# Output projection buffers in one pool laid out by the input projection's bytes, with the last products written in place

## The chip, the cores and the metric

The kernel runs on one core of a Trainium2 chip. The metric is device time in microseconds (us) of one execution; lower is better. The profile is one execution seen by the hardware profiler; its span runs from the first to the last instruction.

## The reference, cut to what matters

One layer over x of 512 tokens by 2048 channels, all in float32:

```python
proj = rmsnorm(x) @ w_in              # 512 x 6144: q, k, v, g_sb, x_lru, g_lru
y_sb  = stick_breaking_attention(q, k, v) * silu(g_sb)     # 8 heads x 128
y_lru = rg_lru(causal_conv(x_lru)) * silu(g_lru)           # 8 groups x 128
out = x + concat(y_sb, y_lru) @ w_out                      # 512 x 2048 @ 2048 x 2048
```

The mixer's result y has 16 tiles of 128 channels by 512 tokens: tiles 0 to 7 are the attention heads, 8 to 15 the recurrent (lru) groups.

## The kernel before, in words

Every matrix product is made from two-part numbers: an operand is split into a high part (cast to fp32r on ScalarE) and a low part (the difference, on VectorE), and three matmuls (high x high, high x low, low x high) stand for one.

**Input projection and mixer.** The loop over p = 0 to 3 takes two heads and two lru groups at a time. For each p three products run over the whole of x: `qk` (then the attention weights), `xg` (then the two lru groups) and `vg` (then `finish_vg`: gates and attention values). x is kept on chip, split, in 32 tiles xh0, xl0 to xh15, xl15 (64 KB of each partition); each of the twelve products reads them in the order 0 to 15, two pairs to a chunk, and `vg3` is the last. The gated results go to DRAM (`finish_y`, a store into `y_dram`), except heads 6 and 7, which are written straight into the buffer that the output projection reads.

**Four pools on the right side of the memory** belong to the input projection, from the edge inwards: xy (the x tiles, 64 KB), qk (split queries and keys, 18 KB), raw (weights as loaded, 16 KB), wsp (split weights, 16 KB). `proj.close()` gives them back, and the output projection's pools are put over the same bytes: c1 (8 tiles of w_out, 32 KB, at the edge), ya (4 tiles of y, 32 KB), wo (split weights, three of each part) and so (split y, six of each part). A tile of these waits only for the tiles whose bytes it takes (`reuse_waits="tile"`). As c1 and ya together are as large as xy, all the ya tiles lie over the second half of the x tiles.

**Output projection.** It is Strassen's: seven products p1, p3, p5, p7, p2, p6, p4 in this order, of 8 steps each (two column halves m by four depth pieces a). A step splits one piece of weights (`woh` on ScalarE, `wol` on VectorE, 128x1024), with m = 0 also a piece of y (`oh`, `ol`), and makes 12 matmuls of 512 columns (lines 602 to 604). The weight pieces are sums of two blocks of w_out: c1 and c2 are loaded (line 547), and after a step's split GpSimd issues an accumulating DMA (`add_c`, line 551) that adds the block that a later product wants. c2 is read by p3 and p7, then c3 takes its place for p2. p1 reads c1. The residual x comes in 16 loads from ScalarE's queue (line 616).

**Order of the loads.** SyncE's queue takes them in the order written: for a = 0 to 3 c1_0_a, c1_1_a and the two halves of ya_a (line 560), then the second half of ya3 (tiles 14 and 15, line 561), then the eight c2 loads. The order of an engine's instructions is fixed when the program is made (a scheduler with a model of the time places them); on the chip each engine runs its list in order. A DMA from SyncE or ScalarE also waits for an earlier one, as eight of them at most are under way.

Of the kernel before, what the change touches and what calls it, by code (L numbers as in the profile page):

```python
# [8 lines left out]
F32 = mybir.dt.float32  # L9
F32R = mybir.dt.float32r  # L10
# [3 lines left out]
ALU = mybir.AluOpType  # L14
# [7 lines left out]
def hybrid_block_kernel(ctx: ExitStack, tc: tile.TileContext, x, norm_gain, w_in, q_norm_gain,  # L22
# [20 lines left out]
    mixer, proj, heads = ExitStack(), ExitStack(), ExitStack()  # L43
    const = ctx.enter_context(tc.tile_pool(name="const", bufs=1))
    dram = ctx.enter_context(tc.tile_pool(name="dram", bufs=1, space=bass.MemoryType.DRAM))
    xy_pool = proj.enter_context(tc.tile_pool(name="xy", bufs=32, side="right"))
    qk_pool = proj.enter_context(tc.tile_pool(name="qk", bufs=2, side="right"))
    raw_pool = proj.enter_context(tc.tile_pool(name="raw", bufs=4, side="right"))
    wsp = proj.enter_context(tc.tile_pool(name="wsp", bufs=4, side="right"))
    v_pool = mixer.enter_context(tc.tile_pool(name="v", bufs=1))  # L50
# [114 lines left out]
    def prep_x(c, xt):  # L165
        for j in range(2):
            kt = 2 * c + j
            ps = ps_a.tile([P, 512], F32, tag="a", name=f"xp{kt}")
            for tt in range(TT):
                nc.tensor.transpose(ps[:, tt * P:(tt + 1) * P],  # L170
                                    xt[:, tt, j * P:(j + 1) * P], ident)
            h = xy_pool.tile([P, S], F32R, tag="xy", name=f"xh{kt}")
            l = xy_pool.tile([P, S], F32R, tag="xy", name=f"xl{kt}")
            evac_x[c] = nc.scalar.activation(h, ps, AF.Copy, scale=gain[:, kt:kt + 1])
            evac_l[kt] = nc.vector.scalar_tensor_tensor(out=l, in0=ps, scalar=gain[:, kt:kt + 1], in1=h.bitcast(F32),
                                           op0=ALU.mult, op1=ALU.subtract)
            xh.append(h)
            xl.append(l)
# [150 lines left out]
    def silu_gate(g, name):  # L329
        e = silu_sig(g, name, "se")  # L330
        nc.vector.tensor_tensor(out=g, in0=g, in1=e, op=ALU.mult)
        return g
# [1 line left out]
    y_dram = dram.tile([KT, P, S], F32, name="y_dram")  # L334
    late = {}

    def y_tile(k, name):

        if k in late:
            return late[k]  # L340
        return y_pool.tile([P, S], F32, tag="y", name=name)

    def finish_y(k, y):
        if k not in late:
            nc.sync.dma_start(y_dram[k], y)
    woff = [0, 512, 896, 1152]

    def attention_weights(h):
# [58 lines left out]
    def attention_values(h, wt, v, gate):  # L407
        hp = h % 2
        o = ps_a.tile([P, 512], F32, tag="a", name=f"o{h}")
        vh, vl, v3 = v  # L410
        wh, wl, w3 = wt
        hs = slice(hp * P, (hp + 1) * P)
        for kb in range(3):
            ws = slice(woff[kb], woff[kb] + S - 128 * kb)
            for a, b in ((vh, wh), (vh, wl), (vl, wh)):
                nc.tensor.matmul(o[:, 128 * kb:512], lhsT=a[:, kb, hs], rhs=b[:, ws],
                                 start=(kb == 0 and b is wh and a is vh), stop=False, skip_group_check=True)
        nc.tensor.matmul(o[:, 384:512], lhsT=v3[:, hs], rhs=w3, start=False, stop=True, skip_group_check=True)
        y = y_tile(h, f"y{h}")
        nc.vector.tensor_tensor(out=y, in0=o, in1=gate, op=ALU.mult)  # L420
        finish_y(h, y)

    def lru(g, xbank, gbank):
        n = f"l{g}"
# [47 lines left out]
        nc.scalar.activation(q, q, AF.Ln)  # L472
        nc.scalar.activation(q, q, AF.Exp, scale=0.5)
        nc.vector.tensor_tensor(out=ig, in0=ig, in1=q, op=ALU.mult)
        y = y_pool.tile([P, S], F32, tag="y", name=f"y{n}")
        nc.vector.tensor_tensor_scan(out=y, data0=r, data1=ig, initial=0.0, op0=ALU.mult, op1=ALU.add)
        gate = silu_gate(gbank, n)
        nc.vector.tensor_tensor(out=y, in0=y, in1=gate, op=ALU.mult)
        finish_y(8 + g, y)

    def finish_vg(p, banks, wts):
        vh = v_pool.tile([P, 3, 256], F32R, tag="vh", name=f"vh{p}")
        vl = v_pool.tile([P, 3, 256], F32R, tag="vl", name=f"vl{p}")
        v3 = v_pool.tile([P, 256], F32, tag="v3", name=f"v3{p}")
        for tt in range(TT):
            src = banks[tt // 2][:, (tt % 2) * 256:(tt % 2) * 256 + 256]
            r = rtok[:, tt:tt + 1]
            if tt == 3:  # L490
                nc.scalar.activation(v3, src, AF.Copy, scale=r)
                continue
            nc.scalar.activation(vh[:, tt, :], src, AF.Copy, scale=r)
            nc.vector.scalar_tensor_tensor(out=vl[:, tt, :], in0=src, scalar=r, in1=vh[:, tt, :].bitcast(F32),
                                           op0=ALU.mult, op1=ALU.subtract)
        v = (vh, vl, v3)
        gs = [evac(banks[2 + i], f"s{2 * p + i}") for i in range(2)]
        gates = [silu_gate(gs[i], f"s{2 * p + i}") for i in range(2)]
        for i in range(2):
            attention_values(2 * p + i, wts[i], v, gates[i])  # L500
# [32 lines left out]

    proj.close()
    NA = 4
    first = ExitStack()
    c1_pool = first.enter_context(tc.tile_pool(name="c1", bufs=8, side="right", reuse_waits="tile"))
    a_pool = first.enter_context(tc.tile_pool(name="ya", bufs=4, side="right", reuse_waits="tile"))
    wo_pool = first.enter_context(tc.tile_pool(name="wo", bufs=3, side="right", reuse_waits="tile"))
    so_pool = first.enter_context(tc.tile_pool(name="so", bufs=6, side="right", reuse_waits="tile"))  # L540

    w_out_a = w_out[0].rearrange("(b a s p) (h m n) -> s p a b h m n", p=P, s=2, a=NA, h=2, n=512)
    y_dram_a = y_dram.rearrange("(b a s) p t -> p a b s t", s=2, a=NA)

    def load_c(pool, tag, s, h, m, a, name):
        t = pool.tile([P, 2, 512], F32, tag=tag, name=name)
        nc.sync.dma_start(t, w_out_a[s, :, a, :, h, m, :])
        return t

    def add_c(t, s, h, m, a):  # L550
        nc.gpsimd.dma_start(t, w_out_a[s, :, a, :, h, m, :], accum_op=ALU.add)  # L551

    ya = [a_pool.tile([P, 2, 2, 512], F32, tag="ya", name=f"ya{a}") for a in range(NA)]
    c1 = {}
    for a in range(NA):
        for m in range(2):
            c1[m, a] = load_c(c1_pool, "c1", 0, 0, m, a, f"c1_{m}_{a}")
        if a < NA - 1:
            for b in range(2):
                nc.sync.dma_start(ya[a][:, b], y_dram_a[:, a, b])  # L560
    nc.sync.dma_start(ya[3][:, 1], y_dram_a[:, 3, 1])
    late[6], late[7] = ya[3][:, 0, 0, :], ya[3][:, 0, 1, :]
    finish_vg(3, banks, wts)

    mixer.close()
    heads.close()
# [4 lines left out]
                                          reuse_waits="tile"))  # L571

    def split_s(i, a, src):
        h = so_pool.tile([P, 2, 256], F32R, tag="sh", name=f"oh{i}_{a}")
        l = so_pool.tile([P, 2, 256], F32R, tag="sl", name=f"ol{i}_{a}")
        nc.scalar.copy(h, src)  # L576
        nc.vector.tensor_tensor(out=l, in0=src, in1=h.bitcast(F32), op=ALU.subtract)  # L577
        return h, l

    def product(i, pool, tag, src, w, after=None):  # L580


        out = {}
        s = []
        for m in range(2):
            for u in range(2):
                out[m, u] = pool.tile([P, 512], F32, tag=tag, name=f"p{i}_{m}{u}")
            for a in range(NA):
                if m == 0:
                    s.append(split_s(i, a, src[a]))  # L590
                sh, sl = s[a]
                wh = wo_pool.tile([P, 2, 512], F32R, tag="woh", name=f"woh{i}_{m}{a}")
                wl = wo_pool.tile([P, 2, 512], F32R, tag="wol", name=f"wol{i}_{m}{a}")
                nc.scalar.copy(wh, w[m, a])  # L594
                nc.vector.tensor_tensor(out=wl, in0=w[m, a], in1=wh.bitcast(F32), op=ALU.subtract)  # L595
                if after is not None:
                    after(m, a)
                for u in range(2):
                    us = slice(u * P, (u + 1) * P)
                    for j in range(2):  # L600
                        st, sp = a == 0 and j == 0, a == NA - 1 and j == 1
                        nc.tensor.matmul(out[m, u], lhsT=sh[:, j, us], rhs=wh[:, j, :], start=st, stop=False)  # L602
                        nc.tensor.matmul(out[m, u], lhsT=sh[:, j, us], rhs=wl[:, j, :], start=False, stop=False)  # L603
                        nc.tensor.matmul(out[m, u], lhsT=sl[:, j, us], rhs=wh[:, j, :], start=False, stop=sp)  # L604
        return out
# [27 lines left out]
    a12 = [t[:, :, 1, 0:256] for t in ya]  # L633
    a22 = [t[:, :, 1, 256:512] for t in ya]

    p1 = product(1, ps_mm, "mm", a11, c1, add_to(c1, 0, 1))
    c2 = {(m, a): load_c(c2_pool, "c2", 1, 1, m, a, f"c2_{m}_{a}") for m in range(2) for a in range(NA)}
    s7, s3 = [], []
    for a in range(NA):
        s7.append(sa_pool.tile([P, 2, 256], F32, tag="s7", name=f"s7_{a}"))  # L640
# [24 lines left out]
        tt(r22[k], r22[k], p5[k], ALU.subtract)  # L665

    p7 = product(7, ps_o, "o", s7, c2)
    c3 = {(m, a): load_c(c2_pool, "c2", 1, 0, m, a, f"c3_{m}_{a}") for m in range(2) for a in range(NA)}
    f = {}
    for k in MU:  # L670
        f[k] = res("f", f"f_{k[0]}{k[1]}")
# [21 lines left out]
    for k in MU:  # L693
        tt(r21[k], p4[k], r21[k])
        store(r21[k], 1, 0, *k)
    first.close()


# [27 lines left out]
```

## Time and profile before

| | |
|---|---|
| median of 3 runs | 808.15 us (808.1 to 809.76) |
| profiled execution | 807.12 us, span 805.4 us |
| TensorE busy | 776.2 us (96%), mean granted clock 0.985 |
| VectorE, ScalarE busy | 513.9 us (64%), 441.4 us (55%) |
| moved by DMA | 101.40 MB, mean 126 GB/s |

The medians are what is compared; the profiled execution is used for where the time goes. A share of busy time is a mean over stages with different limits, so the profile is read by stages.

### The profile page before, as it was taken

Reading aid. Unit: us, or ns where it says so; the run is one execution under the profiler, and the core shown is the slowest. Engines: PE = TensorE matmul, PEld = TensorE weight load, DVE = VectorE, ACT = ScalarE, POOL = GpSimd, SP = SyncE. Lnnn points to the kernel's source line nnn. Section 1 sums busy time; section 2 is a strip of 40 time slices with the busy share of each in tenths; the row PEclk is TensorE's granted clock in tenths of the full one; section 3 lists DMA queues with packets and bytes.
Section 4 is the critical chain, followed back from the end, with each engine's and each line's share of the span. In section 5 each row is a group of like instructions: output and inputs, shape, how many; then the busy total and the mean of one; then the engine's idle time right before and its main releaser. Section 6 shows DMA issues by size and latency. Waiting matters only on the chain.

```text
span 805.4 us, 10605 instructions
## 1 busy us (share of the span) xinstructions
PE 776.2 (96%) x3847; PEld 652.7 (81%) x3847; DVE 513.9 (64%) x857; ACT 441.4 (55%) x828; POOL 42.3 (5%) x55
## 2 busy tenths in 40 slices
PE   8999999999999999999999999999997488999997
PEld 7888889888888888888889888888996365788886
DVE  3665479772547788344589762548779466776794
ACT  5845577752447858225587742456866144545441
POOL 0000000000000000000000000000001033410220
PEclk9999999999999999999999999999999689999999
DMA  9522322232322222423222333322126999995492
GB/s 292 194 79 79 104 84 77 95 113 94 102 87 71 87 95 82 144 84 99 79 85 79 99 117 105 102 83 78 53 66 170 309 254 260 207 254 151 110 233 76
DMA packets 83240, 101.40 MB, mean 126 GB/s; under 512 B 5282, under 2 KB 61172, under 8 KB 83188
## 3 DMA queue, kind: packets, MB, share of 16 engines
q1 hardware_dynamic: 72180, 79.75, 30.7%
q0 software_dynamic: 8704, 16.78, 11.5%
q10 hardware_dynamic: 2304, 4.20, 1.6%
q8 instruction: 30, 0.49, 0.2%
q14 instruction: 22, 0.18, 0.1%
HBM read 92.84 MB, written 7.86 MB: 125 GB/s over the span
## 4 chain that ended last, share of the span: by engine, by line
PE 89%; DMA 9%; SPq 1%; DVE 0%; ACTq 0%; issue 0%; ACT 0%; DVEq 0%
PE p L603 5%; PE p L604 5%; PE p L602 5%; PE z L360 4%; DMA c<-in_w_out_dram 3%; DMA y_dram<-yl 3%; PE qk0b L282 2%; PE qk0b L283 2%; PE qk0b L284 2%; PE xg0b L283 2%; PE xg3b L284 2%; PE xg2b L284 2%; PE xg1b L284 2%; PE xg0b L284 2%; PE xg2b L282 2%; PE xg3b L282 2%
## 5 line engine op out<-in xcount | busy, mean ns | idle before, releaser
L602 PE MATMUL p<-woh,oh 128*128 128x512 f32 x224 | 82.9, 409 | 18.8 <-ACT oh L576 13.6
L594 ACT CAST woh<-c 128x1024 fp32r<-128x1024 f32 x56 | 58.7, 1049 | 68.4 <-PE p L604 41.6
L595 DVE TENSOR_TENSOR wol<-c,woh 128x1024 fp32r<-128x1024 f32 x56 | 68.2, 1222 | 42.9 <-ACT woh L594 42.9
L603 PE MATMUL p<-wol,oh 128*128 128x512 f32 x224 | 91.0, 406 | 3.6 <-DVE wol L595 3.6
L604 PE MATMUL p<-woh,ol 128*128 128x512 f32 x224 | 88.7, 401 | 0.0
L602 PEld LDWEIGHTS p<-woh,oh 128*128 128x128 f32 x224 | 43.5, 196 | 31.3 <-ACT oh L576 14.7
L603 PEld LDWEIGHTS p<-wol,oh 128*128 128x128 f32 x224 | 43.9, 196 | 16.3 <-DVE wol L595 7.3
L551 POOL DMA_DIRECT2D c<-in_w_out_dram x32 | 38.7, 1211 | 262.0 <-DVE ql L471 138.7
L604 PEld LDWEIGHTS p<-woh,ol 128*128 128x128 f32 x224 | 43.7, 195 | 9.2 <-DVE ol L577 0.2
L372 ACT ACTIVATE sp<-z 128x128 f32<-128x128 f32 (+3 forms) x32 | 13.9, 434 | 25.1 <-PE z L360 24.9
L283 PE MATMUL qk0b<-xl,hqk 128*128 128x512 f32 x64 | 26.4, 413 | 0.0
L284 PE MATMUL qk0b<-xh,lqk 128*128 128x512 f32 x64 | 25.2, 394 | 0.0
L283 PE MATMUL xg0b<-xl,hxg 128*128 128x512 f32 x64 | 25.2, 394 | 0.0
L282 PE MATMUL xg1b<-xh,hxg 128*128 128x512 f32 x64 | 25.1, 393 | 0.0
L282 PE MATMUL xg2b<-xh,hxg 128*128 128x512 f32 x64 | 25.1, 393 | 0.0
L282 PE MATMUL xg3b<-xh,hxg 128*128 128x512 f32 x64 | 25.1, 393 | 0.0
L282 PE MATMUL xg0b<-xh,hxg 128*128 128x512 f32 x64 | 25.1, 392 | 0.0
L283 PE MATMUL xg1b<-xl,hxg 128*128 128x512 f32 x64 | 25.1, 392 | 0.0
L283 PE MATMUL xg2b<-xl,hxg 128*128 128x512 f32 x64 | 25.1, 392 | 0.0
L283 PE MATMUL xg3b<-xl,hxg 128*128 128x512 f32 x64 | 25.1, 392 | 0.0
L284 PE MATMUL qk1b<-xh,lqk 128*128 128x512 f32 x64 | 25.0, 390 | 0.0
L576 ACT CAST oh<-ya 128x512 fp32r<-128x512 f32 x20 | 12.4, 621 | 22.9 <-PE p L603 14.7
(442 smaller groups left out, 2307.0 us busy)
## 6 DMA issues: line engine op xcount, KB each, us to landing
c<-in_w_out_dram POOLq DMA_DIRECT2D x32, 512.0 KB, 12.3
c<-in_w_out_dram SPq DMA_DIRECT2D x24, 512.0 KB, 9.8
qk0r<-in_w_in_dram SPq DMA_DIRECT2D x16, 256.0 KB, 4.9
xg0r<-in_w_in_dram SPq DMA_DIRECT2D x16, 256.0 KB, 2.9
vg0r<-in_w_in_dram SPq DMA_DIRECT2D x16, 256.0 KB, 3.1
qk1r<-in_w_in_dram SPq DMA_DIRECT2D x16, 256.0 KB, 2.9
xg1r<-in_w_in_dram SPq DMA_DIRECT2D x16, 256.0 KB, 2.8
vg1r<-in_w_in_dram SPq DMA_DIRECT2D x16, 256.0 KB, 3.0
```

Of the source, the lines that this page charges most:

```text
L282: nc.tensor.matmul(banks[b], lhsT=wh[:, cs], rhs=xh[kt], start=st, stop=False)
L283: nc.tensor.matmul(banks[b], lhsT=wh[:, cs], rhs=xl[kt], start=False, stop=False)
L284: nc.tensor.matmul(banks[b], lhsT=wl[:, cs], rhs=xh[kt], start=False, stop=sp)
L360: nc.tensor.matmul(o, lhsT=lhsT, rhs=rhs, start=start, stop=stop, skip_group_check=True)
L372: nc.scalar.activation(e, z, AF.Abs)
L551: nc.gpsimd.dma_start(t, w_out_a[s, :, a, :, h, m, :], accum_op=ALU.add)
L576: nc.scalar.copy(h, src)
L594: nc.scalar.copy(wh, w[m, a])
L595: nc.vector.tensor_tensor(out=wl, in0=w[m, a], in1=wh.bitcast(F32), op=ALU.subtract)
L602: nc.tensor.matmul(out[m, u], lhsT=sh[:, j, us], rhs=wh[:, j, :], start=st, stop=False)
L603: nc.tensor.matmul(out[m, u], lhsT=sh[:, j, us], rhs=wl[:, j, :], start=False, stop=False)
L604: nc.tensor.matmul(out[m, u], lhsT=sl[:, j, us], rhs=wh[:, j, :], start=False, stop=sp)
```

## The change

The pool qk moves to the right edge, and the x tiles go into four pools of eight (xy0 to xy3, four pairs each). The output projection gets one pool, `op`, with one slot for each buffer, listed in an order made by hand; the split y tiles have 4 slots of both parts (s0 to s3) instead of 6 and 6, the split weights 3 slots of both parts. The pools are now, from the edge: qk 18 KB, xy0, xy1, xy2, xy3 of 16 KB each, raw, wsp; read from its end, the list goes ya0, c1_0_0, ya3, s0, wo0, ya1, c1_0_1, s1, wo1, ya2, wo2, c1_0_2, c1_0_3, s2, s3, c1_1_0 to c1_1_3. The loads are issued in another order: ya0 to ya2 each followed by its c1_0_a, c1_0_3, and the four c1_1_a behind `finish_vg(3)`. Tiles 14 and 15 are no longer stored and loaded again: like 6 and 7 they are multiplied by their gates straight into ya3, and all four multiplications are written down later than before.

```diff
-    xy_pool = proj.enter_context(tc.tile_pool(name="xy", bufs=32, side="right"))
     qk_pool = proj.enter_context(tc.tile_pool(name="qk", bufs=2, side="right"))
+    xy_pools = [proj.enter_context(tc.tile_pool(name=f"xy{i}", bufs=8, side="right")) for i in range(4)]
...
+    def gated(k, y, gate):
+        if k in (6, 7, 14, 15):
+            late[k] = (y, gate)
+            return
+        out = y_pool.tile([P, S], F32, tag="y", name=f"y{k}") if k < 8 else y
+        nc.vector.tensor_tensor(out=out, in0=y, in1=gate, op=ALU.mult)
+        nc.sync.dma_start(y_dram[k], out)
...
-    c1_pool = first.enter_context(tc.tile_pool(name="c1", bufs=8, side="right", reuse_waits="tile"))
-    a_pool = first.enter_context(tc.tile_pool(name="ya", bufs=4, side="right", reuse_waits="tile"))
-    wo_pool = first.enter_context(tc.tile_pool(name="wo", bufs=3, side="right", reuse_waits="tile"))
-    so_pool = first.enter_context(tc.tile_pool(name="so", bufs=6, side="right", reuse_waits="tile"))
+    op_pool = ctx.enter_context(tc.tile_pool(name="op", bufs=1, side="right", reuse_waits="tile"))
+    slots = {}
+    for tag, cols in ((["c1_1_3", 1024], ["c1_1_2", 1024], ["c1_1_1", 1024], ["c1_1_0", 1024], ["s3", 1024],
+                       ["s2", 1024], ["c1_0_3", 1024], ["c1_0_2", 1024], ["wo2", 2048], ["ya2", 2048],
+                       ["wo1", 2048], ["s1", 1024], ["c1_0_1", 1024], ["ya1", 2048], ["wo0", 2048],
+                       ["s0", 1024], ["ya3", 2048], ["c1_0_0", 1024], ["ya0", 2048])):
+        slots[tag] = cols
...
     for a in range(NA):
-        for m in range(2):
-            c1[m, a] = load_c(c1_pool, "c1", 0, 0, m, a, f"c1_{m}_{a}")
-        if a < NA - 1:
+        if a < 3:
             for b in range(2):
                 nc.sync.dma_start(ya[a][:, b], y_dram_a[:, a, b])
-    nc.sync.dma_start(ya[3][:, 1], y_dram_a[:, 3, 1])
-    late[6], late[7] = ya[3][:, 0, 0, :], ya[3][:, 0, 1, :]
+        load_c(c1[0, a], 0, 0, 0, a)
+    for k in (14, 15):
+        y, gate = late[k]
+        nc.vector.tensor_tensor(out=ya[3][:, 1, k - 14], in0=y, in1=gate, op=ALU.mult)
     finish_vg(3, banks, wts)
+    for k in (6, 7):
+        y, gate = late[k]
+        nc.vector.tensor_tensor(out=ya[3][:, 0, k - 6], in0=y, in1=gate, op=ALU.mult)
+    for a in range(NA):
+        load_c(c1[1, a], 0, 0, 1, a)
...
     def split_s(i, a, src):
-        h = so_pool.tile([P, 2, 256], F32R, tag="sh", name=f"oh{i}_{a}")
-        l = so_pool.tile([P, 2, 256], F32R, tag="sl", name=f"ol{i}_{a}")
+        t = held.pop(f"s{a}") if i == 1 else op_tile(f"s{a}", F32R, f"os{i}_{a}")
+        t = t.rearrange("p (x b n) -> p x b n", x=2, b=2)
+        h, l = t[:, 0], t[:, 1]
```

## Rows read from the trace of the kernel before

**Rows 1.** Stages: PE, PEld, DVE, ACT, POOL busy; granted clock, DMA share, GB/s.

```profile
600.00:612.00 12.00, 12.00 (x72) 10.74 (x72) 8.52 (x16) 11.39 (x22) 0.00 (x0) 1.00 0.03 6
612.00:642.00 30.00, 16.37 (x52) 12.39 (x50) 19.90 (x30) 8.59 (x13) 3.74 (x3) 0.72 1.03 305
642.00:650.00 8.00, 2.81 (x7) 1.65 (x6) 3.25 (x4) 3.04 (x3) 2.30 (x2) 0.69 0.58 179
690.00:705.00 15.00, 15.00 (x67) 12.36 (x67) 13.03 (x17) 7.21 (x8) 8.46 (x7) 1.00 1.13 206
690.00:800.00 110.00, 110.00 (x486) 91.02 (x486) 81.30 (x95) 49.24 (x55) 20.50 (x17) 1.00 0.77 174
612.00:690.00 78.00, 55.56 (x199) 40.28 (x198) 48.55 (x65) 29.65 (x41) 18.18 (x15) 0.85 1.01 270
```

**Rows 2.** TensorE in time: last of the mixer, first and last of the output projection.

```profile
613.68 0.39 PE L418 MATMUL o<-w,v 128*128 128x128 f32 x2
617.75 0.79 PE L602 MATMUL p<-woh,oh 128*128 128x512 f32 x1 [3.68 <-ACT oh L576]
...
800.80 0.39 PE L604 MATMUL p<-woh,ol 128*128 128x512 f32 x1
```

**Rows 3.** The page's groups: first matmul of a step, and the split of y.

```profile
L602 PE MATMUL p<-woh,oh 128*128 128x512 f32 x224 | 82.9, 409 | 18.8 <-ACT oh L576 13.6
...
L576 ACT CAST oh<-ya 128x512 fp32r<-128x512 f32 x20 | 12.4, 621 | 22.9 <-PE p L603 14.7
```

**Rows 4.** SyncE's queue in time, around the end of the mixer.

```profile
592.75 0.94 SPq L547 DMA_DIRECT2D c<-in_w_out_dram  x2
610.51 0.88 SPq L560 DMA_DIRECT2D ya<-y_dram  x2
...
645.50 0.37 SPq L561 DMA_DIRECT2D ya<-y_dram  x1
645.97 17.76 SPq L547 DMA_DIRECT2D c<-in_w_out_dram  x8
```

**Rows 5.** The chain that ended last, 605 to 700 us: start, length, what.

```profile
623.65 21.79 DMA y_dram<-yl
...
662.53 24.79 DMA c<-in_w_out_dram
...
695.11 0.45 PE p L602 x2
...
697.83 0.45 PE p L602 x2
```

**Rows 6.** ScalarE in time: the first and last of five weight casts that wait for c2.

```profile
671.41 1.05 ACT L594 CAST woh<-c 128x1024 fp32r<-128x1024 f32 x1 [2.64 <-DMA c<-in_w_out_dram]
...
687.42 1.05 ACT L594 CAST woh<-c 128x1024 fp32r<-128x1024 f32 x1 [2.47 <-DMA c<-in_w_out_dram]
```

**Rows 7.** TensorE: last readers of key 7, of x pair 11 and of x pair 15.

```profile
L360 PE MATMUL z<-q7h,k7l x1: 391/391/391, 588.2 to 588.2; 128*128 128x512 f32 x1
...
597.59 0.40 PE L284 MATMUL vg3b<-xh,lvg 128*128 128x512 f32 x1
...
610.09 0.40 PE L284 MATMUL vg3b<-xh,lvg 128*128 128x512 f32 x1
```

**Rows 8.** VectorE in time: the last late product and a weight split.

```profile
629.04 0.68 DVE L420 TENSOR_TENSOR ya<-o,vs 128x512 f32<-128x512 f32 x1
631.62 1.22 DVE L595 TENSOR_TENSOR wol<-c,woh 128x1024 fp32r<-128x1024 f32 x1 [1.89 <-ACT woh L594]
```

**Rows 9.** DMA issues from 590 to 700 us: count, KB each, median us to landing.

```profile
c<-in_w_out_dram SPq DMA_DIRECT2D x16, 512.0 KB, 13.4
...
r<-in_x_dram ACTq DMA_DIRECT2D x12, 256.0 KB, 4.2
```

**Rows 10.** Who waited for whom from 690 us on: total, times, longest.

```profile
ACT oh L576 <- PE p L603: 18.0, 15, 1.4
...
PE p L603 <- DVE wol L595: 0.5, 1, 0.5
```

More of the change, by code (lines that the diff above doesn't have):

```diff
@@ L171, in prep_x @@
                                     xt[:, tt, j * P:(j + 1) * P], ident)
-            h = xy_pool.tile([P, S], F32R, tag="xy", name=f"xh{kt}")
-            l = xy_pool.tile([P, S], F32R, tag="xy", name=f"xl{kt}")
+            h = xy_pools[kt // 4].tile([P, S], F32R, tag="xy", name=f"xh{kt}")
+            l = xy_pools[kt // 4].tile([P, S], F32R, tag="xy", name=f"xl{kt}")
             evac_x[c] = nc.scalar.activation(h, ps, AF.Copy, scale=gain[:, kt:kt + 1])
@@ L335, in hybrid_block_kernel @@
     late = {}
[L337 to L345, printed above, removed]
+    def gated(k, y, gate):
[5 more added lines that the diff above has]
+        nc.sync.dma_start(y_dram[k], out)
     woff = [0, 512, 896, 1152]
@@ L418, in attention_values @@
         nc.tensor.matmul(o[:, 384:512], lhsT=v3[:, hs], rhs=w3, start=False, stop=True, skip_group_check=True)
-        y = y_tile(h, f"y{h}")
-        nc.vector.tensor_tensor(out=y, in0=o, in1=gate, op=ALU.mult)
-        finish_y(h, y)
+        gated(h, o, gate)
     def lru(g, xbank, gbank):
@@ L474, in lru @@
         nc.vector.tensor_tensor(out=ig, in0=ig, in1=q, op=ALU.mult)
-        y = y_pool.tile([P, S], F32, tag="y", name=f"y{n}")
+        y = y_pool.tile([P, S], F32, tag="y", name=f"h{n}")
         nc.vector.tensor_tensor_scan(out=y, data0=r, data1=ig, initial=0.0, op0=ALU.mult, op1=ALU.add)
-        gate = silu_gate(gbank, n)
-        nc.vector.tensor_tensor(out=y, in0=y, in1=gate, op=ALU.mult)
-        finish_y(8 + g, y)
+        gated(8 + g, y, silu_gate(gbank, n))
     def finish_vg(p, banks, wts):
@@ L535, in hybrid_block_kernel, with op_tile, load_c @@
     NA = 4
-    first = ExitStack()
-    c1_pool = first.enter_context(tc.tile_pool(name="c1", bufs=8, side="right", reuse_waits="tile"))
-    a_pool = first.enter_context(tc.tile_pool(name="ya", bufs=4, side="right", reuse_waits="tile"))
-    wo_pool = first.enter_context(tc.tile_pool(name="wo", bufs=3, side="right", reuse_waits="tile"))
-    so_pool = first.enter_context(tc.tile_pool(name="so", bufs=6, side="right", reuse_waits="tile"))
+    op_pool = ctx.enter_context(tc.tile_pool(name="op", bufs=1, side="right", reuse_waits="tile"))
+    slots = {}
+    for tag, cols in ((["c1_1_3", 1024], ["c1_1_2", 1024], ["c1_1_1", 1024], ["c1_1_0", 1024], ["s3", 1024],
[3 rows of a table added]
+        slots[tag] = cols
+    def op_tile(tag, dtype, name):
+        return op_pool.tile([P, slots[tag]], dtype, tag=tag, name=name)
     w_out_a = w_out[0].rearrange("(b a s p) (h m n) -> s p a b h m n", p=P, s=2, a=NA, h=2, n=512)
     y_dram_a = y_dram.rearrange("(b a s) p t -> p a b s t", s=2, a=NA)
-    def load_c(pool, tag, s, h, m, a, name):
-        t = pool.tile([P, 2, 512], F32, tag=tag, name=name)
+    def load_c(t, s, h, m, a):
         nc.sync.dma_start(t, w_out_a[s, :, a, :, h, m, :])
@@ L551, in add_c @@
         nc.gpsimd.dma_start(t, w_out_a[s, :, a, :, h, m, :], accum_op=ALU.add)
-    ya = [a_pool.tile([P, 2, 2, 512], F32, tag="ya", name=f"ya{a}") for a in range(NA)]
-    c1 = {}
+    held = {tag: op_tile(tag, F32R if tag[0] in "sw" else F32, f"{tag}_") for tag in slots}
+    ya = [held[f"ya{a}"].rearrange("p (b s t) -> p b s t", b=2, s=2) for a in range(NA)]
+    c1 = {(m, a): held[f"c1_{m}_{a}"].rearrange("p (b n) -> p b n", b=2) for m in range(2) for a in range(NA)}
     for a in range(NA):
-        for m in range(2):
-            c1[m, a] = load_c(c1_pool, "c1", 0, 0, m, a, f"c1_{m}_{a}")
-        if a < NA - 1:
+        if a < 3:
             for b in range(2):
                 nc.sync.dma_start(ya[a][:, b], y_dram_a[:, a, b])
-    nc.sync.dma_start(ya[3][:, 1], y_dram_a[:, 3, 1])
-    late[6], late[7] = ya[3][:, 0, 0, :], ya[3][:, 0, 1, :]
+        load_c(c1[0, a], 0, 0, 0, a)
+    for k in (14, 15):
+        y, gate = late[k]
+        nc.vector.tensor_tensor(out=ya[3][:, 1, k - 14], in0=y, in1=gate, op=ALU.mult)
     finish_vg(3, banks, wts)
+    for k in (6, 7):
[3 more added lines that the diff above has]
+        load_c(c1[1, a], 0, 0, 1, a)
     mixer.close()
@@ L578, in split_s @@
         return h, l
+    turn = iter(range(1000))
     def product(i, pool, tag, src, w, after=None):
@@ L591, in product @@
                 sh, sl = s[a]
-                wh = wo_pool.tile([P, 2, 512], F32R, tag="woh", name=f"woh{i}_{m}{a}")
-                wl = wo_pool.tile([P, 2, 512], F32R, tag="wol", name=f"wol{i}_{m}{a}")
+                n = next(turn)
+                wt = held.pop(f"wo{n}") if n < 3 else op_tile(f"wo{n % 3}", F32R, f"wo{i}_{m}{a}")
+                wt = wt.rearrange("p (x b n) -> p x b n", x=2, b=2)
+                wh, wl = wt[:, 0], wt[:, 1]
                 nc.scalar.copy(wh, w[m, a])
@@ L634, in hybrid_block_kernel, with c2_tile @@
     a22 = [t[:, :, 1, 256:512] for t in ya]
+    def c2_tile(name):
+        return c2_pool.tile([P, 2, 512], F32, tag="c2", name=name)
     p1 = product(1, ps_mm, "mm", a11, c1, add_to(c1, 0, 1))
-    c2 = {(m, a): load_c(c2_pool, "c2", 1, 1, m, a, f"c2_{m}_{a}") for m in range(2) for a in range(NA)}
+    c2 = {(m, a): load_c(c2_tile(f"c2_{m}_{a}"), 1, 1, m, a) for m in range(2) for a in range(NA)}
     s7, s3 = [], []
@@ L667, in hybrid_block_kernel @@
     p7 = product(7, ps_o, "o", s7, c2)
-    c3 = {(m, a): load_c(c2_pool, "c2", 1, 0, m, a, f"c3_{m}_{a}") for m in range(2) for a in range(NA)}
+    c3 = {(m, a): load_c(c2_tile(f"c3_{m}_{a}"), 1, 0, m, a) for m in range(2) for a in range(NA)}
     f = {}
@@ L695, in hybrid_block_kernel @@
         store(r21[k], 1, 0, *k)
-    first.close()
 _INS = ["x", "norm_gain", "w_in", "q_norm_gain", "k_norm_gain", "conv_w", "conv_b", "lru_w_a", "lru_b_a",
```

## The prediction, made before the changed kernel was run

> **What bounds the kernel now.** I read the stages first. TensorE is busy all of the time up to 612 us and again from 690 on (110.00 us of 110), at a granted clock of 1.00 [rows 1]. Between them it is busy 55.56 us of 78, while the DMA engines are full (share 1.01, 270 GB/s), but for a lull at 642 to 650 us with 179 GB/s; and just ahead of it, at 600 to 612 us, they are idle (share 0.03) [rows 1]. So the stage in which time is lost comes right behind one in which the DMA could have worked.
>
> How much is lost: the output projection has 7 x 8 = 56 steps of 12 matmuls, and two steps follow each other 697.83 - 695.11 = 2.72 us apart where nothing waits [rows 5]. That is 152.3 us of work. TensorE ends the mixer at 614.1 and starts its last matmul at 800.8, which is some 187 us [rows 2]. The difference, 34.6 us, is the most that any better feeding can give back. As the five products behind p3 run without a gap, p3 now ends at 801.0 - 40 x 2.72 = 692.2; all the loss lies in p1 and p3.
>
> Why: the first matmul of a step waits 18.8 us in all, 13.6 of it for `oh`, the split of y [rows 3]. The first ya load is issued only at 610.51, since ya lies over x tiles that are read until 610.09 [rows 4, 7]. The c1 loads behind it in the queue wait as well, though their bytes were free long before. Then ya3 waits for tile 15, stored and read back: the store is under way 21.79 us behind the other loads, ya3 is issued at 645.50, and the eight c2 loads stand behind it and start at 645.97 [rows 4, 5]. The last c2 lands at 662.53 + 24.79 = 687.3, and p3's last step goes on from there [rows 5]. The clock falls too: 0.72 in 612 to 642 us, behind such waits [rows 1].
>
> **The change, part by part.**
>
> *Where the buffers lie.* ya0 and c1_0_0 take bytes of qk, last read at 588.2 (TensorE, key 7). ya1 and c1_0_1 lie over xy1 and the rim of xy0, ya2 over xy2, whose last reader is at 597.59; c1_0_2 and c1_0_3 lie over xy3 and wait until 610.09 as ya does today [rows 7]. Today's first c1 load goes out at 592.75 [rows 4], behind the store of tile 14, and that store goes away. So ya0, c1_0_0, ya1, c1_0_1 can start at about 588.6 and ya2 at about 598: eight loads of 512 KB, 4.2 MB, some 15 us at 280 GB/s (worked out below). They should have landed by about 607, inside a stage where TensorE is the bound and the DMA idle [rows 1]. Today two loads land ahead of 610 (c1_0_0 and c1_1_0) [rows 4]; after, eight.
>
> *What leaves the full stage.* Of the 78 x 0.270 = 21.1 MB moved from 612 to 690 us [rows 1], seven ya loads of a c load's size, 0.524 MB [rows 9] (six, of line 560, move ahead; the seventh, of line 561, is dropped) and the store of tile 15 (0.262 MB by its shape) go: 3.93 MB. The c1 loads cancel: six are left behind 610 before and after. 17.1 MB stay: 6 c1, 8 c2, 12 residual loads [rows 9] and about 12 accumulating DMAs. Without the lull (which the round trip of tile 15 makes, and that is gone) the rate is (21.06 - 8 x 0.179) / 70 = 280 GB/s, so 17.1 MB take 61.2 us instead of 78: 16.8 us saved.
>
> *The same from the other side.* At the end of p3 the casts that wait for c2 come every (687.42 - 671.41) / 4 = 4.00 us [rows 6]: a c2 load and an accumulating one share the engines. Six c1 loads (3.15 MB, 11.2 us at 280 GB/s) from 612, eight c2 at 4.0 us, and the 12 residual loads of 256 KB (3.15 MB, 11.2 us) give 612 + 11.2 + 32 + 11.2 = 666.4 for the last c2, against 687.3: 20.9 us saved. The two differ by how many of p3's accumulating DMAs (0.524 MB at 206 GB/s, about 2.5 us each [rows 1]) come in ahead of the last c2; I see nothing that decides it, and take the middle, 19 us.
>
> A rule would price this otherwise. The Trainium skill, "DMA: Bandwidth & Descriptors", section "Specifications", gives about 358 GB/s as the HBM limit of a core; by that figure 17.1 MB would take 48 us and the saving would be an estimated 30 us. The trace speaks against it for this mix: with the engines full, accumulating DMAs run at 206 GB/s [rows 1].
>
> *Does anything else bind first?* TensorE: from 614.1, sixteen steps of 2.72 us end at 657.6, ahead of 671. VectorE: behind 614 it has about ten operations of the mixer, 16 sums of y for p3, p5 and p7, four `ol` (some 0.68 us each [rows 8]) and eight `wol` of 1.22: 30 x 0.68 + 9.8 = 30 us, so p1 ends near 645 at the earliest if all of it comes ahead; p3 at full pace then ends at 667. That is close below the DMA's 671 to 675 (last c2 plus the 4.9 us that lie behind it today), but below it.
>
> *Products in place.* The four multiplications stay (0.68 us each [rows 8]); two stores and a load go. y7 was ready at 629.04 + 0.68, held up by VectorE's own waits for ya; it should be ready near 625. p1's step with ya3 can be passed by the m = 1 steps, as it is today.
>
> *Four slots for split y.* Before, two pieces of the next product could be split at any time. Now piece a waits until the current product's step (m = 1, a) is done. That is three steps, 8.2 us, ahead of its use, for 0.62 + 0.68 us of work [rows 3, 8]. Already now the `oh` casts wait 18.0 us on TensorE in 15 waits from 690 on, and TensorE itself lost 0.5 us [rows 10]. I cost it at nothing; its cover is that distance. If the cover is gone, a product loses at most the two splits of y and of weights that follow one another, 0.62 + 1.05 + 0.68 + 1.22 = 3.6 us [rows 3, 6, 8], or 21.4 us for six products.
>
> *One tile for both parts of a weight split; four x pools; list order.* Same operations, same third-last step to wait for: nothing.
>
> **Sum.** 805.4 - 19 = 786.4 us of span. The profiled run took 807.12, 1.7 above its span, and the median is 1.0 above that, so I predict 808.15 - 19 = **789.2 us**.
>
> **Rivals.**
>
> *A. The DMA keeps up (12%).* If fewer accumulating DMAs stand between the c2 loads, p1 and p3 run at TensorE's pace and the whole 34.6 us come back: 773.5 us. For it: loads alone reach over 300 GB/s (305 in 612 to 642) [rows 1]. Against it: the steady 4.00 us [rows 6]. By the 358 GB/s of the Trainium skill's "DMA: Bandwidth & Descriptors", "Specifications", it would be an estimated 778.
>
> *B. The c2 loads stay late (11%).* The residual loads, ScalarE's, wait for their turn among at most eight transfers, and ScalarE's casts wait behind them; if they come first, c2 ends some 10 us later than I say: 797 to 800 us.
>
> *C. The change doesn't do what it says (7%).* The trace does not show at which end of the pool the list begins. If ya0 lay at the far end (over wsp, read until 610.09), every load would still start at 610.5, and only the round trip of tile 15 would be saved: 0.79 MB (2.8 us) and the lull, 8 x (280 - 179) / 280 = 2.9 us. That is 802.5 us.
>
> *D. The slots bind (6%): slower.* The 3.6 us of splits come exposed once in each of six products, as ScalarE's and VectorE's lists are in fixed order. 21.4 us lost against 19 won: 810.5 us. It decides from 3.2 us a product on. Against it: 8.2 us of distance. For it: VectorE is busy 81.30 us of 110 there [rows 1], in bunches.
>
> **How the numbers follow.** My case (61%) gives 782 to 796, the two sums with two accumulating DMAs on either side. A range from 777 to 802 leaves out most of A, half of C, D and an unchanged time (3%): about 2 in 10. Differences under 0.2% (1.6 us) are what these runs can't tell from no change. Faster: my case, A, B and C, 0.91; same 0.03; slower 0.06.
>
> **What would show it.** ya0's first load issued near 589 instead of 610.5; the DMA busy at 590 to 607; a first gap of TensorE behind 614 under 3.68 us and no wait for `oh` on a ya load; a granted clock near 1.00 at 612 to 642; the first c2 load issued by about 625; casts of p3 still waiting for c2 some 4 us apart; p3 ending at 671 to 675; from there 108.8 us of TensorE without gaps. I am wrong if p3 ends with no wait for c2 (A), if ScalarE sits on line 616 while casts are due (B), if ya0 goes out at 610 (C), or if TensorE has waits for `oh` in p5 to p4 (D).

## The result, and the profile after

The changed kernel takes **800.87 us** (median of 4 runs, 799.62 to 802.18) against 808.12 us for the kernel before in the same comparison: a ratio of 0.9909, 95% interval 0.9884 to 0.9933. It is faster, by 7.3 us or 0.9%; the prediction said 19 us. The profiled execution took 799.62 us, with a span of 797.9.

The stages of the kernel after (columns as in [rows 1]):

```profile
580.00:600.00 20.00, 20.00 (x124) 17.93 (x124) 15.82 (x31) 11.62 (x23) 0.00 (x0) 1.00 0.48 163
600.00:612.00 12.00, 12.00 (x74) 10.78 (x73) 8.70 (x16) 10.62 (x20) 0.00 (x0) 1.00 0.30 94
612.00:642.00 30.00, 23.16 (x93) 17.71 (x92) 27.99 (x41) 14.04 (x20) 8.55 (x7) 0.89 1.04 274
650.00:660.00 10.00, 0.00 (x0) 0.00 (x0) 0.00 (x0) 0.81 (x1) 0.00 (x0) 0.55 1.10 254
660.00:670.00 10.00, 9.68 (x33) 7.35 (x34) 7.18 (x8) 6.75 (x10) 4.81 (x4) 0.76 1.06 249
670.00:680.00 10.00, 10.00 (x46) 8.29 (x45) 8.42 (x12) 4.44 (x5) 4.49 (x4) 1.00 1.11 201
690.00:790.00 100.00, 100.00 (x443) 82.81 (x442) 73.36 (x87) 46.21 (x52) 15.65 (x13) 1.00 0.73 166
```

The first two lines show the change at work: the DMA engines, idle at 600 to 612 us before, now move data from 588 on. The third shows TensorE busy 23.16 us of 30 where it had 16.37. The fourth is the surprise: for ten microseconds no engine but ScalarE computes anything, and that only for 0.81 us. What happens there is seen in the queues and lists. SyncE's queue of the kernel after, in time (to be held against [rows 4]):

```profile
588.42 0.88 SPq L562 DMA_DIRECT2D ya__6059<-y_dram  x2
...
609.65 0.37 SPq L549 DMA_DIRECT2D c__6048<-in_w_out_dram  x1
...
614.75 16.39 SPq L549 DMA_DIRECT2D c<-in_w_out_dram  x8
```

ScalarE of the kernel after, in time, with the DMAs that it issues (ACTq):

```profile
642.88 1.05 ACT L608 CAST wo<-c__6041 128x1024 fp32r<-128x1024 f32 x1 [5.34 <-DMA c<-in_w_out_dram]
...
647.69 11.40 ACTq L630 DMA_DIRECT2D r<-in_x_dram  x5
659.19 1.04 ACT L608 CAST wo<-c 128x1024 fp32r<-128x1024 f32 x1 [14.74 <-DMA r<-in_x_dram]
```

Two of these issues by themselves, and TensorE behind them:

```profile
653.00 0.33 ACTq L630 DMA_DIRECT2D r<-in_x_dram  x1
...
657.77 1.32 ACTq L630 DMA_DIRECT2D r<-in_x_dram  x3
...
660.29 1.22 PE L616 MATMUL p<-wo,os 128*128 128x512 f32 x2 [12.48 <-ACT wo L608]
```

The eight c2 loads of line 549, first and last start, and their time to landing (the longest is that of the last):

```profile
L549 SPq DMA_DIRECT2D c<-in_w_out_dram x8: 367/803/2337, 614.7 to 628.8; - x8
...
DMA to landing us min/median/max: 10.1/11.5/29.0
```

Read from below: p3's first matmul waits for ScalarE's cast of its first weights (line 608); the cast stands in ScalarE's list behind residual loads (line 630); such a load is issued only when an earlier load has landed, and those that were under way were the c2 loads, issued by SyncE at 614.75 to 631. The trace has the landing of each: the last four c2 loads landed at 642.41, 647.67, 652.98 and 657.75 (628.8 + 29.0), and ScalarE's loads went out at 642.43, 647.69, 653.00 and 657.77. With two more behind that one it was through at 659.09, and the cast started at 659.19. (The profile names a residual load as what ended the cast's wait of 14.74 us, but the cast reads none; what it stood behind is the list.) So the c2 loads, brought forward by 31 us, took the turns that the residual loads needed, and ScalarE stood on those for 11.40 us with p3's casts behind them.

TensorE lost 34.8 us before, counted from the start of the mixer's last matmul to the start of the last of all, less 152.3 us of work [rows 2] (the prediction's 34.6 us are counted from the mixer's end). The same count from the trace after (613.51 and 793.04) is 27.2 us. Of these 12.48 us are the gap at 660.29, and some 2.4 us the low clock behind it: from 660.29 to the start of the last matmul are 132.75 us, of which p3 and the five products behind it need 130.3. In 660 to 670 us TensorE made 33 matmuls at a granted clock of 0.76, where ten microseconds at 1.00 hold 46.

### The profile page after: what moved, and what is told of

It is laid out like the page before. It is cut to its first block, busy times and chain, and to the rows that moved or that the text cites. A ratio compares the mean times of both kernels' runs of the same rounds, so it can differ in the third digit from the quotient of the medians.

```text
span 797.9 us, 10584 instructions
## 1 busy us (share of the span) xinstructions
PE 770.3 (97%) x3847; PEld 650.6 (82%) x3847; DVE 512.4 (64%) x857; ACT 441.1 (55%) x828; POOL 42.3 (5%) x55
## 4 chain that ended last, share of the span: by engine, by line
PE 92%; DMA 5%; DVE 1%; issue 0%; SPq 0%; ACT 0%; DVEq 0%
PE p L616 6%; PE p L617 6%; PE p L618 6%; PE z L360 4%; DMA c<-in_w_out_dram 3%; PE qk0b L282 2%; PE qk0b L283 2%; PE xg0b L283 2%; PE qk0b L284 2%; PE xg1b L284 2%; PE xg2b L284 2%; PE xg3b L284 2%; PE xg0b L284 2%; PE xg3b L282 2%; PE xg1b L282 2%; PE xg2b L282 2%
## 5 line engine op out<-in xcount | busy, mean ns | idle before, releaser
L616 PE MATMUL p<-wo,os 128*128 128x512 f32 x192 | 67.5, 394 | 12.5 <-ACT wo L608 12.5
L617 PE MATMUL p<-wo,os 128*128 128x512 f32 x192 | 75.6, 394 | 0.0
L618 PE MATMUL p<-wo,os 128*128 128x512 f32 x192 | 75.4, 393 | 0.0
L616 PEld LDWEIGHTS p<-wo,os 128*128 128x128 f32 x192 | 36.5, 190 | 20.4 <-ACT wo L608 12.9
L608 ACT CAST wo<-c 128x1024 fp32r<-128x1024 f32 x24 | 25.2, 1050 | 45.0 <-PE p L618 29.1
L609 DVE TENSOR_TENSOR wo<-c,wo 128x1024 fp32r<-128x1024 f32 x24 | 29.4, 1224 | 32.0 <-ACT wo L608 31.9
L617 PEld LDWEIGHTS p<-wo,os 128*128 128x128 f32 x192 | 36.4, 190 | 8.3 <-DVE wo L609 0.8
L618 PEld LDWEIGHTS p<-wo,os 128*128 128x128 f32 x192 | 36.5, 190 | 7.6
L282 PE MATMUL qk2b<-xh,hqk 128*128 128x512 f32 x64 | 24.9, 389 | 0.0
L282 PE MATMUL qk3b<-xh,hqk 128*128 128x512 f32 x64 | 24.9, 389 | 0.0
```

The costliest lines, as they stand in the source:

```text
L282: nc.tensor.matmul(banks[b], lhsT=wh[:, cs], rhs=xh[kt], start=st, stop=False)
```

## The experiments

A table first; the last column is TensorE's loss, counted as above from each run's own trace. Each was timed beside the kernel before on its chip (medians 806.7 to 807.0 us; the kernel after beside one of 808.12), so that a difference between two rows is good to a microsecond or so.

| kernel | median us | ratio to before, 95% | loss us |
|---|---|---|---|
| before | 808.12 | | 34.8 |
| after | 800.87 | 0.9909 (0.9884 to 0.9933) | 27.2 |
| r_on_sync | 796.44 | 0.9870 (0.9845 to 0.9894) | 23.8 |
| r_behind_p3 | 794.19 | 0.9841 (0.9817 to 0.9864) | 20.6 |
| old_bytes | 809.88 | 1.0036 (1.0021 to 1.0051) | 34.6 |
| tile15_through_dram | 806.21 | 0.9990 (0.9974 to 1.0006) | 34.5 |
| no_residual | 784.08 | 0.9713 (0.9683 to 0.9743) | 11.7 |
| x_late | 785.63 | 0.9720 (0.9689 to 0.9751) | 11.7 |
| before_r_on_sync | 810.41 | 1.0040 (1.0024 to 1.0056) | 37.0 |
| before_x_late | 795.49 | 0.9868 (0.9824 to 0.9912) | 21.4 |
| x_late_sums_later | 780.10 | 0.9667 (0.9653 to 0.9682) | 6.7 |
| r_ahead_of_c2 | 799.39 | 0.9900 (0.9872 to 0.9928) | 25.5 |

### First four: the residual loads' place, and the two halves of the change

Theory S was that ScalarE's list, held by the residual loads, took the missing 12 us; theory D that the bytes of the stage did. **r_on_sync** issues the residual loads from SyncE, behind the c2 loads; **r_behind_p3** leaves them on ScalarE, behind p3's last weight cast.

```diff
 r_on_sync:
-        nc.scalar.dma_start(t, x2[ts, ns])
+        nc.sync.dma_start(t, x2[ts, ns])
 r_behind_p3:
-                nc.scalar.copy(wh, w[m, a])
+                casts[i] = nc.scalar.copy(wh, w[m, a])
...
-        nc.scalar.dma_start(t, x2[ts, ns])
+        with tc.issue_after(casts[3].ins):
+            nc.scalar.dma_start(t, x2[ts, ns])
```

> The changed kernel with one edit: the 16 loads of the residual go out from SyncE's queue instead of ScalarE's. ScalarE's list of casts stays as it is. Theory S (ScalarE's list): behind p1, ScalarE stands 11.4 us on residual loads that wait for their turn among eight transfers, and p3's first cast stands behind them (TensorE idle 12.48 us ahead of 660.29). Then p3 starts near 648, unless single casts wait for c2, and the time is 786 to 791 us. Theory D (the bytes, my prediction's): the DMA engines are full up to 690 us anyway, p3's casts would then wait for c2 instead, and the time stays within 2 us of 800.9.

> The changed kernel with one edit: the residual loads stay on ScalarE's queue, but are placed behind the last weight cast of p3 in its list. Theory S: as they no longer stand ahead of p3's casts, p3 starts near 648 and the time is 784 to 791 us; sums with the residual come later, and cost nothing as p7 is the next to want those PSUM banks. Theory D: 799 to 803 us, p3's casts waiting for c2. If this one is fast and the one on SyncE's queue is not, it is a matter of the queue.

Measured: 796.44 and 794.19 us, 4.4 and 6.7 us less than after: more than D allows, less than S wanted. The stall was not taken away but moved. In r_on_sync ScalarE is free and p3 runs at full pace up to its last step, but there VectorE stands, in the same kind of list: its sums of p3, which want the residual's data, are ahead of the split of p3's last weights. TensorE's wait in r_on_sync, then VectorE in time:

```profile
PE p L617 <- DVE wo L609: 10.1, 1, 10.1
```

```profile
675.37 0.69 DVE L640 TENSOR_TENSOR r<-r,e 128x512 f32<-128x512 f32 x1 [11.45 <-DMA r<-in_x_dram]
```

In r_behind_p3 both happen, smaller (ScalarE 6.30 us on an issue in p5, TensorE 4.79 us on VectorE at 691). So the theory had to be widened: not ScalarE's list alone, but any list in order that needs the residual loads between 640 and 690 us (theory L below).

**old_bytes** puts the pools back as they were (xy at the edge, then qk, and a list of slots to match); the late products stay in place. **tile15_through_dram** stores tiles 14 and 15 and loads them again; the new layout stays.

```diff
 old_bytes:
-    for tag, cols in ((["c1_1_3", 1024], ["c1_1_2", 1024], ["c1_1_1", 1024], ["c1_1_0", 1024], ["s3", 1024],
...
+    for tag in ("s3", "s2", "s1", "s0", "wo2", "wo1", "wo0", "ya0", "ya3", "ya2", "ya1", "c1_1_3", "c1_0_3",
+                "c1_1_2", "c1_0_2", "c1_1_1", "c1_0_1", "c1_1_0", "c1_0_0"):
 tile15_through_dram:
-        if k in (6, 7, 14, 15):
+        if k in (6, 7):
...
+    nc.sync.dma_start(ya[3][:, 1], y_dram_a[:, 3, 1])
```

> The changed kernel with the bytes as before: x tiles at the edge, c1 over their first half, ya over their second half, the split buffers over qk, raw and wsp. Loads in the new order, tiles 14 and 15 in place, four slots of split y. So the loads ahead of 610 us go, and what is left is the end of the round trip of tile 15. Theory S: the early loads of y are worth the start of p1 only (it starts at about 617 in both kernels), and p3 is held by the residual loads in both: 800 to 805 us. Theory D: all of the layout's 4 MB come back into the full stage, 14 us more than with the new bytes, so above 808 us.

> The changed kernel with tiles 14 and 15 stored to DRAM and loaded into ya3 again, behind the four late c1 loads, as before the change; bytes and the order of all other loads as in the changed kernel. The c2 loads stand behind the load of ya3 again, which waits for tile 15's store. Theory S: c2 starts some 20 us later (near 640), so p3 waits for it as well as for the residual loads: 804 to 809 us, most of the gain gone. Theory D: 0.79 MB and a lull more, 5 to 6 us: 805 to 808 us. The two don't differ here; the run says which part of the change the gain comes from.

Measured: 809.88 and 806.21 us. Neither half of the change is worth anything by itself (old_bytes is even 0.36% slower than before). The number of old_bytes falls on theory D's side, and that of the other tells nothing apart. SyncE of old_bytes, then of tile15_through_dram:

```profile
610.84 0.88 SPq L559 DMA_DIRECT2D ya__6048<-y_dram  x2
```

```profile
641.29 0.37 SPq L570 DMA_DIRECT2D ya__6061<-y_dram  x1
645.56 18.21 SPq L549 DMA_DIRECT2D c<-in_w_out_dram  x8
```

With the old bytes no y load starts ahead of 610.84, as before, and the c2 loads start at 625.39; with the round trip the eight c2 loads stand behind tile 15's load until 645.56, as before. Only both together bring the c2 loads to 614.75. But the bytes alone don't explain old_bytes: ScalarE stood on residual loads there too, with TensorE idle for 10.73 us behind it.

```profile
649.73 12.39 ACTq L627 DMA_DIRECT2D r<-in_x_dram  x4
662.24 1.04 ACT L605 CAST wo<-c__6052 128x1024 fp32r<-128x1024 f32 x1 [14.58 <-DMA c<-in_w_out_dram]
```

### The residual loads left out, or needed late

**no_residual** adds tiles that are there in place of x, so that its output lacks x. **x_late** keeps every byte and the result: x of the quarters 12 and 22 goes into the bytes of s3 and s7 once p3 and p7 have read them, that of 11 behind the last c3 load, and the sums are made when there is time.

```diff
 x_late:
-        r12[k] = load_res("r12", f"r12_{k[0]}{k[1]}", 0, 1, *k)
-        tt(r12[k], p3[k], r12[k])
-        tt(r12[k], r12[k], e1[k], ALU.subtract)
+        r12[k] = res("r12", f"r12_{k[0]}{k[1]}")
+        tt(r12[k], p3[k], e1[k], ALU.subtract)
...
+            x[k] = sa_pool.tile([P, 512], F32, tag=tag, name=f"x{i}_{k[0]}{k[1]}")
+            ts, ns = place(i, 1, *k)
+            nc.sync.dma_start(x[k], x2[ts, ns])
```

> The kernel after without the 16 residual loads: where x was added, a tile that is there already (e1 or f) is added instead, so that every engine but the DMA has the same operations, and the output lacks x. Theory L (the residual loads hold engines that work in order: ScalarE where they are issued, VectorE where their data are due): nothing holds p3 or p5 any more; TensorE starts p1 near 614.5, works 152.3 us and loses some 9.5 us in p1 (6.8 us idle and 3 us at the lower clock, as in the run with the residual loads behind p3), so the last matmul ends near 777 and the time is 781 to 785 us. Theory D (the bytes of the stage hold it): 4.2 MB less are worth some of that too, but the accumulating DMAs of p1 and p3 and the c2 loads are as many as before, so p3 or p5 should now show waits for them: 786 to 792.

> The kernel after with the residual's bytes kept and only their due time moved: the x tiles of the quarters 12 and 22 are loaded by SyncE into the bytes of s3 and s7, which p3 and p7 have read, behind the c2 loads, and are added in p6; those of the quarter 11 are loaded behind the last c3 load and added behind p2. ScalarE issues no load ahead of p6 and VectorE waits for none in p3 and p5; VectorE has four operations more. Theory L: as without the loads, 781 to 787 us. Theory D: the 2.1 MB or so that are still moved between 645 and 690 us take some 8 us of full DMA engines from the accumulating DMAs that p5 waits for: 789 to 796.

Measured: 784.08 and 785.63 us. Theory L holds for both. The 1.5 us between them are less than the scatter of either (783.53 to 786.76, 782.98 to 786.46): where x_late puts the bytes, they cost nothing that these runs show. Stages of x_late:

```profile
616.00:620.00 4.00, 1.22 (x2) 0.50 (x2) 4.00 (x8) 3.59 (x7) 0.00 (x0) 0.68 0.97 341
640.00:660.00 20.00, 20.00 (x90) 16.57 (x89) 13.09 (x15) 10.73 (x15) 8.79 (x9) 1.00 1.10 256
660.00:690.00 30.00, 30.00 (x134) 24.86 (x133) 21.15 (x25) 14.78 (x18) 13.00 (x11) 1.00 1.13 208
```

From 640 us on the DMA engines are as full as ever (share 1.10 and 1.13), and TensorE has no gap at all. Full engines are not a bound if nothing waits for their last byte.

### The same edits on the kernel before

> The kernel before with the one edit of the residual loads issued by SyncE in place of ScalarE. In it ScalarE stood on these loads as well (12 us near 630 to 645), but its casts in p3 waited for the c2 loads until 687. Theory L: the hold is covered by the late c2 loads, no change, 805 to 809 us; only the change uncovers it. If the hold costs the same whatever the rest does, the gain is the 4 us that the same edit gave in the kernel after: 802 to 804.

> The kernel before with the same edit as x_late (x of the quarters 12, 22 and 11 loaded late by SyncE, no load on ScalarE ahead of p6). Theory L: in the kernel before the late c2 loads hold p3 whether or not ScalarE stands on residual loads, so nothing is gained by taking them away: 804 to 809 us; the change is then worth 19 to 23 us between this kernel and x_late (785.6), which is what the prediction had summed up for it. If the residual loads were the common bound of both kernels, the edit would give here the 15 us that it gave there: about 792.

Measured: 810.41 us for the one-line edit, outside both ranges (3.5 us slower than the kernel before beside it: the loads now stand in SyncE's queue ahead of ya3's last half and c2, and TensorE waits 15.38 us for the split of ya3), and 795.49 us for the late x. The second refutes what I expected: the residual loads held the kernel before too, by 11.2 us. How is seen on ScalarE of before_x_late, in two of its casts that wait for c2 (to be held against [rows 6]):

```profile
664.04 1.05 ACT L596 CAST woh<-c 128x1024 fp32r<-128x1024 f32 x1 [3.00 <-DMA c<-in_w_out_dram]
...
676.00 1.05 ACT L596 CAST woh<-c 128x1024 fp32r<-128x1024 f32 x1 [2.38 <-DMA c<-in_w_out_dram]
```

The casts still come some 4 us apart, but the last that waits comes at 676.00 and not at 687.42, 11.4 us earlier, and 3.15 MB at the prediction's 280 GB/s are 11.2 us. So in the kernel before the residual loads were bytes ahead of the c2 loads (this rests on the two numbers agreeing; ScalarE also stood there for some 12 us, and no run takes the two apart); in the kernel after the c2 loads are ahead, and the residual loads hold a list. With neither in the way the change is worth 795.49 - 785.63 = 9.9 us.

### The order that the prediction's sum had assumed

**r_ahead_of_c2** issues the twelve residual loads from SyncE ahead of the c2 loads, in the kernel after.

```diff
+    for tag, i, j in (("r12", 0, 1), ("r22", 1, 1), ("r11", 0, 0)):
+        for k in MU:
+            first[tag, k] = load_res(tag, f"{tag}_{k[0]}{k[1]}", i, j, *k)
...
+            with tc.issue_after(last.ins):
+                c2[m, a] = load_c(t, 1, 1, m, a)
```

> The kernel after with the 12 residual loads of the quarters 12, 22 and 11 issued by SyncE ahead of the c2 loads, in which order the prediction's sum took them (and near which they stand in the kernel before); the sum of the quarter 11 behind p2's last split, so that VectorE's list has no other work ahead of p3. Theory P (the prediction's own sum: the last c2 lands behind c1, c2 and 3.15 MB of residual loads): the c2 loads are issued some 10 us later, the last lands at 664 to 668 instead of 653, p3's casts wait for c2 some 4 us apart, p3 ends at 671 to 675, and the time is 787 to 792 us. Theory L (only lists that are held cost time, the order of the bytes does not): no list is held, so 783 to 787.

Measured: 799.39 us: neither. SyncE, then ScalarE of this run:

```profile
625.05 15.99 SPq L633 DMA_DIRECT2D r<-in_x_dram  x12
641.14 17.57 SPq L549 DMA_DIRECT2D c<-in_w_out_dram  x8
```

```profile
659.31 1.04 ACT L609 CAST wo<-c 128x1024 fp32r<-128x1024 f32 x1 [10.34 <-DMA c<-in_w_out_dram]
660.63 1.05 ACT L609 CAST wo<-c 128x1024 fp32r<-128x1024 f32 x1 [0.28 <-DMA c<-in_w_out_dram]
662.00 1.05 ACT L609 CAST wo<-c 128x1024 fp32r<-128x1024 f32 x1 [0.32 <-DMA c<-in_w_out_dram]
665.30 1.05 ACT L609 CAST wo<-c 128x1024 fp32r<-128x1024 f32 x1 [2.25 <-PE p L619]
```

The residual loads started only at 625.05, and the c2 loads were issued 26 us later than in after, not 10. p3's first cast waits for the first c2, and TensorE has a gap of 12.58 us, as long as that of after. Against theory P the wait is at the start of p3, not at its last pieces, and from 665.30 on the casts follow TensorE, not c2. Against L as it stands on record, the order of the loads costs time though neither ScalarE nor VectorE is held: the list that stands here is SyncE's, with the c2 loads behind the residual loads in it.

The casts also show what made 4 us of a c2 load. Here three of them come 1.3 us apart, each released by a c2 load, and GpSimd's list says why (issues of accumulating DMAs, then the stage):

```profile
642.85 1.20 POOL L553 DMA_DIRECT2D c__6041<-in_w_out_dram  x1 [0.53 <-DVE wo L610]
662.14 3.68 POOL L553 DMA_DIRECT2D c<-in_w_out_dram  x3 [18.10 <-DVE wo L610]
```

```profile
659.00:664.60 5.60, 4.16 (x10) 2.91 (x11) 3.68 (x3) 3.14 (x3) 2.44 (x2) 0.56 1.05 396
```

The last accumulating DMA of p1 landed at 658.98, the next at 672.04; the five c2 loads that landed from 659.23 to 664.62 had the engines to themselves. In before and before_x_late the c2 loads land 4 us apart with accumulating DMAs landing all the while, at first p1's and then p3's. So the prediction's reading of the 4.00 us, that a c2 load and an accumulating one share the engines, holds.

### What is left in p1

In x_late and no_residual the whole loss of 11.7 us lies ahead of 634 us; TensorE's only waits from 612 us on in x_late are shown below. **x_late_sums_later** moves the sums of y on VectorE behind p1's weight splits.

```diff
-        tt(s7[a], a11[a], a21[a], ALU.subtract)
-        tt(a21[a], a22[a], a21[a], ALU.subtract)
...
+        with tc.issue_after(subs[1, 1, a].ins):
+            tt(s7[a], a11[a], a21[a], ALU.subtract)
...
+    for a in range(NA):
+        with tc.issue_after(subs[3, 1, 2].ins):
+            tt(a21[a], a22[a], a21[a], ALU.subtract)
```

> x_late, with the sums of y for p3, p5 and p7 moved on VectorE: those of p3 and p7 behind p1's splits of the m = 1 weights instead of between those of m = 0, those of p5 into p3. The same operations. Theory V (VectorE, busy without a gap from 612 to 640, is what p1 now waits for): four operations of some 0.6 us leave the way ahead of each of p1's first two weight splits, and p1 loses some 3 to 5 us less: 780 to 783 us. If p1's loss lies in its first wait (3.04 us) and the lower clock behind it, or if p3 then waits for the sums: 784 to 788.

Measured: 780.10 us, 5.5 us less than x_late, at the low end of theory V. TensorE's waits for VectorE shrink; x_late, then this run (total, times, longest):

```profile
PE p L619 <- ACT wo__6055 L611: 3.0, 1, 3.0
PE p L620 <- DVE wo__6051 L612: 2.0, 1, 2.0
PE p L620 <- DVE wo__6055 L612: 1.3, 1, 1.3
PE p L619 <- ACT wo L611: 0.7, 1, 0.7
```

```profile
PE p L619 <- ACT wo__6055 L611: 2.6, 1, 2.6
PE p L620 <- DVE wo__6051 L612: 0.7, 1, 0.7
PE p L620 <- DVE wo__6055 L612: 0.6, 1, 0.6
```

The waits fall from 7.0 to 3.9 us; of the 5.0 us of loss that go, the rest goes with the clock (the granted clock in 620 to 624 us was 0.50 in x_late and 0.69 here). This version beats both kernels: the kernel before by 3.3%, and the kernel after, going by the two ratios, by 2.4%.

## Why the prediction was right and wrong

**Right: where the buffers lie.** The first y load went out at 588.42 (said: near 589), the first c2 load at 614.75 (said: by 625), TensorE's first gap behind the mixer fell to 3.04 us, and no split of y waits for a load. Rival C is out.

**Right: the slots.** From 690 to 790 us TensorE is busy 100.00 us of 100; nothing waits for a split of y. The cost of nothing stands, and rival D is out. p1's lower bound by VectorE was also met: it ended at 660.29 - 12.48 = 647.8, and VectorE was busy 27.99 us of 30. The clock rose from 0.72 to 0.89, not to 1.00.

A smaller miss: y7, said to be ready near 625, was ready at 635.31; TensorE had no wait from 631 to 643 us.

**Wrong: what the last c2 costs.** "What leaves the full stage" and "the same from the other side" both put p3's end behind the landing of the last c2, the second at 666.4. It landed at 657.75, 8.6 us sooner, and no cast of p3 waited for a c2 load at all, let alone every 4.00 us. The pace was sized well: in x_late the last four c2 loads landed 4.0 us apart and the last at 654.85, where the sum without residual loads gives 612 + 11.2 + 32 = 655.2. The term that was mis-sized is the 11.2 us of residual bytes. The c2 loads were now issued by 631, ahead of all residual loads, and only six of the twelve had landed by then: the last c2 came 2.6 us behind that sum, not 11.2. And p3 wants its last weights later than that: in x_late they are cast at 662.60, so c2 was no longer the bound.

**Wrong: the step "Does anything else bind first?".** It asked TensorE and VectorE, and left out ScalarE's list and the turn-taking of the loads. That is where the time went: p3 should have ended at 671 to 675 and ended at 793.43 - 40 x 2.72 = 684.6, held by 12.48 us of gap and some 2.4 us of clock, 14.9 in all. x_late, which loads and needs the residual later, gains 800.87 - 785.63 = 15.2 us (14.0 by the kernels before beside them), and its p3 ends at 779.52 - 108.8 = 670.7, beside the 671 to 675 of the prediction, but by p1's end (648.8) and eight steps of TensorE, not by c2. Rival B had this mechanism, and its sign, ScalarE on residual loads while casts are due, is what the trace shows; its range of 797 to 800 us lies next to the 800.87 measured. It was given 11%, and its reason (c2 ends later) was the wrong way round. Rival A's sign, p3 without a wait for c2, came true as well, but not its time.

**A right sum for a wrong reason.** That x_late lands within the likeliest case (782 to 796) doesn't rescue the 19 us: between kernels that both load the residual late the change is worth 9.9 us. The prediction's baseline had, unnoticed, some 11 us in it that the residual loads cost and that the change alone could not remove.

**Rates.** The Trainium skill, "DMA: Bandwidth & Descriptors", section "Specifications", gives about 358 GB/s as a core's HBM limit. The trace does not keep to it where loads run alone: in r_ahead_of_c2 they moved 396 GB/s from 659 to 664.6 us, and in x_late, before its first accumulating DMA, 341 at 616 to 620. With accumulating DMAs among them the full engines moved 208 GB/s at 660 to 690 in x_late. For this mix the trace's rate is the price, as the prediction took it. (The 305 GB/s that rival A calls "loads alone" are not: GpSimd issued three accumulating DMAs in that stretch, POOL x3 in [rows 1].)

**Open.** Whether the 11 us of the kernel before are the residual's bytes alone, or in part ScalarE's stand on its loads, was not taken apart.

## What to carry to other kernels

When loads are brought forward, write down what they now stand in front of: where queues share their turns, as here, the loads that lose theirs hold the whole list of the engine that issues them, and an engine that does compute on the critical path is a bad place to issue from. Moving such a load to another queue moves the wait; what removes it is needing the data later. And before a saving is summed, take the suspected common bound out of both kernels: it shows what the change is worth and what was never its to give.

## What the runs showed of the hardware

A wait of TensorE costs more than its length: the granted clock was 0.55 from 650 to 660 us, inside the gap of 12.48 us, and 0.76 over the ten microseconds behind it, so partly at the lower of its two levels (1.2 of 2.4 GHz), which added some 2.4 us.

DMA engines at a share of 1.10 to 1.13 for 50 us, in x_late, cost TensorE nothing. And a full share says little of the rate: it was 396 GB/s with loads alone (share 1.05) and 208 with accumulating DMAs (1.13).
